# A hybrid attention/SSD trunk layer: later DMA landings in the kernel's own instruction planner, and range checks without a written place on ScalarE

## The chip, the cores and the metric

The kernel runs on one core of a Trainium2 chip. The metric is the device time of one execution in microseconds; the number for a kernel is the median of its runs. A trace comes from one more execution under the hardware profiler, and its span is counted from the first to the last instruction of the kernel.

## What is computed

One layer for 1,024 prompt tokens and 8 x 16 sample tokens, with a model width of 1,024. Cut to what matters here:

```python
def trunk_layer(x, c, conv_buf, h0, attn_fn, norm_g, w_ada, b_ada, w_in, q_norm_g, k_norm_g,
                w_att_proj, conv_w, conv_b, dt_bias, a_log, d_skip, ssd_norm_g, w_ssd_proj, w_out):
    mod = jax.nn.silu(c) @ w_ada + b_ada
    shift, scale, gate = jnp.split(mod[:, None, :], 3, axis=-1)
    h = rms_norm(x, norm_g) * (1 + scale) + shift
    proj = h @ w_in
    q, k, v, z_att, z_ssd, xbc, dt_raw, gates = jnp.split(proj, IN_SPLITS, axis=-1)
    ...
    o_att, k_st, v_st = attn_fn(q, k, v)
    att_branch = (o_att.reshape(b, s, ATT_WIDTH) * jax.nn.silu(z_att)) @ w_att_proj
    xbc, conv_new = causal_dwconv(xbc, conv_buf, conv_w, conv_b)
    ...
    y, h_new = ssd_scan(xs_h, dt, a, bm, cm, h0)
    y = y * jax.nn.silu(z_ssd)
    y = rms_norm(y, ssd_norm_g)
    ssd_branch = y @ w_ssd_proj
    g_att, g_ssd = jnp.split(gates, 2, axis=-1)
    merged = jax.nn.sigmoid(g_att) * att_branch + jax.nn.sigmoid(g_ssd) * ssd_branch
    out = x + gate * (merged @ w_out)
    return out, k_st, v_st, conv_new, h_new
```

All inputs are float32. The attention is chunk-banded (own chunk and the eight chunks of 64 tokens before it), the SSD branch is a Mamba-2 scan in chunks of 64.

## The kernel before, in words

**Arithmetic.** A float32 operand of a large product is cut into two float16 halves: ScalarE writes the high half (L697 for weights, L2198 for operands), VectorE the low half (L698, L2200), and TensorE adds three products, high x high, high x low, low x high (L970, L971, L973 in `dense`; L1023 to L1025 in `dense_tok`; L876 to L878 in `quad_dense`). Since float16 has a small range, each weight and each operand also has its mean square taken: `level` (L689) runs one Square activation on ScalarE with an accumulator, and at the very end all sums are looked at to decide whether a second, general kernel in the same program has to run. It doesn't run with these inputs. Nothing but that last decision waits for a check; only the buffer that it reads stays taken until it has read it.

**Stages.** From 0 to about 83 us the modulation, the normalised input h (`h_hi` L1160, `h_rest` L1165, `h_smp` L1169) and the first product. The weight of that first product (w01) and the three parts of the next are cut by hand there (`w01_high` L1185, `w_high` L1226, `w_low2` L1232), the columns of the modulation come from `mod_cols` L1102, `mod_copy` L1127, `mod_sum` L1108, `mod_c` L1138 and L1139. From there to about 600 us eight attention units (the in-projection of one unit, L1023 to L1025, its evictions L1464, L1465, L1467, its transposes L1521 on TensorE behind a GpSimd multiply L1501). From 600 to about 1264 us sixteen pairs of SSD heads (`dense`, L970 to L973, beside the scan, L1804 to L2151). From 1264 us to the end the two merge gates, the two branch projections and the output projection. These are done with seven products of half-size blocks where the plain way has eight (`quad_dense`, L876 to L878, kept partial sums L895, joined sums L901), for which sums of weight blocks are needed: `quad_sums` loads a weight during the SSD stage (L704), adds its blocks on VectorE (L708) and stores the sums to memory (`sum_d`, L712); they are loaded again just before use (L679). The operands of that stage come back from memory as well (`y_d`, L2281), are multiplied on VectorE (L2286) and cut (L2198, L2200).

**What sets the order.** The code emits all instructions in a written order. A planner in Python, `class Order`, then puts them in the order that is run. `build` makes units of them (one instruction each; up to three matmuls of one tile are merged) with the edges between them. `run` walks through a simulated time: each engine takes, among the units whose inputs are there, first those whose inputs have been there for a safety margin, and of these the one with the smallest number `at`. A unit in the set `fill` has 600 added to its number, so others go first; one in `fast` has 300 taken off. An instruction that the code wraps in `late` is pinned: it gets an edge to the instruction written just before it on its engine, so it keeps that place. For a DMA the plan reckons with a landing of `bus + 700` (L386 to L388). `apply` then fixes the order of every engine by edges, and semaphores between the engines do the rest. So a number in the planner moves no work in or out; it only changes the order in which an engine takes its instructions, and an instruction that has to wait on its engine holds up all that stand behind it.

**Queues.** SP issues all loads, GpSimd the stores to memory that are read again. TensorE has the accumulators `d` (3 slots), `g` (3) and `s` (1) in PSUM: a new tile waits until an old one of its kind has been evicted.

Of the kernel before, what the change touches and what calls it, by code (L numbers as in the profile page):

```python
# [59 lines left out]
SW = 2.0 ** 8  # L60
# [76 lines left out]
        self.arena.release(self.at)  # L137


class Order:  # L140


# [9 lines left out]
    def __init__(self, tc, instructions, pinned, cuts, slow, fill, fast):  # L152
        self.tc, self.slow, self.fill, self.fast = tc, slow, fill, fast
        self.list = [x for x in instructions if x.opcode != "TilePoolBoundary"]
        self.pinned, self.cuts = pinned, cuts

    @staticmethod
    def engine(x):
# [74 lines left out]
    def build(self):  # L233

        units, self.of, last = [], {}, None
        for x in self.list:
            e = self.engine(x)
            if e == "PE":
                small = x.tile_size[0] * x.tile_size[1] < 16384
                out = x.outs[0].bass_ap.tensor.name  # L240
                key = (small, tuple(x.tile_size), "" if small else out)
                if last and last["key"] == key and x.name not in self.cuts and (small or len(last["ins"]) < 3):
                    last["ins"].append(x)
                    self.of[x.name] = last
                    continue
            u = {"eng": e, "ins": [x], "i": len(units), "pred": {}, "succ": [], "key": None}
            if e == "PE":
                u["key"] = key
                last = u
            units.append(u)  # L250
            self.of[x.name] = u
# [4 lines left out]
        for x in self.list:  # L256
            u = self.of[x.name]
            e = u["eng"]
# [4 lines left out]
            for a, w in acc:  # L263
                t, name, r0, r1, c0, c1 = self.region(a)
# [54 lines left out]
    def run(self):  # L319
# [10 lines left out]
        order = {e: [] for e in engines}  # L330
        key = [None]
        bus, low, done = 0.0, 0, [False] * len(units)
# [21 lines left out]
        while n < len(units):  # L354
            best = None
            for e in engines:
# [12 lines left out]
                t = max(free[e], min(c))  # L369
                if best is None or t < best[0]:  # L370
                    best = (t, e)
            assert best, ("no unit can go on", [(e, [(u["i"], u["ins"][0].name) for u in ready[e]][:4]) for e in engines])
            t, e = best
            can = [u for u in ready[e] if u["now"] <= t and u["i"] < low + self.AHEAD]
            sure = [u for u in can if u["sure"] <= t]
# [6 lines left out]
            if u["dma"]:  # L382
                k = nlane[e] % 8
                nlane[e] += 1
                t = max(t, lanes[e][k])
                bus = max(t + 1400, bus) + lat  # L386
                lanes[e][k] = bus + 700
                lat = bus + 700 - t  # L388
            busy = u["busy"]
            if e == "PE":  # L390
                g = u["key"][1]
# [34 lines left out]
def trunk_kernel(ctx: ExitStack, tc: tile.TileContext, h, again):  # L426
# [258 lines left out]
    def level(x, scale, keep=lambda x: x, kind="w"):  # L685

        c, n = meant[kind], x.shape[-1]
        meant[kind] += 1
        keep(nc.scalar.activation(junk[:, :n], x, AF.Square, scale=scale * n ** -0.5, accum_out=sums[:, c:c + 1]))  # L689
# [538 lines left out]
    def w_low2(j):  # L1228
        hi, lo, _ = wsplit[1]
        b = wraw.pop(1 + j)  # L1230
        c = slice(j * 1024, (j + 1) * 1024)
        late(nc.vector.scalar_tensor_tensor(lo.r[:, c], b.ap, SW, hi.ap[:, c], ALU.mult, ALU.subtract))  # L1232
        level(b.ap, SW, late)
        b.free()


    for k in range(KT):
        if k == 0:
# [15 lines left out]
            mod_copy(2)  # L1254
            h_rest(1)
            w01_low(slice(256, 1024))
            level(wraw[0].ap, SW, late)
            wraw.pop(0).free()
            z_mm(0, 0, hlo)
            mod_b(2)  # L1260
# [173 lines left out]
    def h_level():  # L1434
        for k in range(KT):
            yield from pause(6000)
            level(hhi[k].r, 1.0, kind="x")

    urgent.append(ev_first())
    urgent.append(h_level())  # L1440
# [1024 lines left out]
    items.append((out_dense(), [], [], 0.5))  # L2465
    run(items)
    order = Order(tc, list(nc.cur_bb.bb.instructions), pinned, cuts, slow, fill, fast)
    order.build()
    order.run()
    order.apply()  # L2470


# [1866 lines left out]
```

## Time and profile before

| | us |
|---|---|
| median of 3 runs | 1724.09 (1721.27 to 1725.70) |
| the profiled execution's own time | 1723.17 |
| its span in the trace | 1721.4 |
| TensorE matmuls busy | 1678.6 |
| VectorE busy | 1376.6 |
| ScalarE busy | 1058.1 |
| GpSimd busy | 369.1 |

What lies outside the span is 1723.17 - 1721.4 = 1.8 us. In rows of the trace a bracket such as [1.02 <-POOL arena L1501] says that the engine was idle for 1.02 us just before this instruction, and which instruction released it. Names in front of an arrow are the tile that is written: `arena` is the working memory, `d`, `g` and `s` are PSUM tiles. PE is TensorE, DVE is VectorE, ACT is ScalarE, POOL is GpSimd, SP issues the loads.

### The profile page before, as it was taken

The page shows a single profiled execution, that of the slowest core. Times are in us where ns is not written, and L with a number is a line of the kernel's source. Part 1 is how long each engine was busy: PE and PEld are TensorE (multiplying, and loading weights), DVE is VectorE, ACT ScalarE, POOL GpSimd, SP SyncE. Part 2 cuts the span into 40 slices and gives each one's busy share as a digit, 9 for nine tenths or more (in the row PEclk, how much of TensorE's full clock was granted, in tenths as well). Part 3 has the DMA queues.
Part 4 walks back from the last instruction along what each step waited for, and adds up shares of the span by engine and source line. Part 5 has one row for each costly group of instructions (what it writes and reads, how often), then busy time and mean ns, then how long its engine had stood idle before and what let it go on. Part 6 is the DMA issues. An engine that isn't in the chain of part 4 may idle for free. (4 is left out here: it accounts for less than half of the span.)

```text
span 1721.4 us, 36659 instructions
## 1 busy us (share of the span) xinstructions
PE 1678.6 (98%) x14265; PEld 1120.4 (65%) x14265; DVE 1376.6 (80%) x2539; ACT 1058.1 (61%) x2123; POOL 369.1 (21%) x640
## 2 busy tenths in 40 slices
PE   7999999999999999999999999999999999999998
PEld 3556565556565556666666666666657777777776
DVE  6458767878877888889988998997798677888973
ACT  8766556566565668457655765665379665774550
POOL 0133233135133111322321232232212101010000
PEclk9999999999999999999999999999999999999999
DMA  9248789797978687676858867788756866687661
GB/s 383 82 122 210 170 228 225 168 232 187 219 219 192 165 199 221 181 221 199 194 172 263 241 194 238 235 216 268 284 198 221 274 240 234 232 287 264 224 212 65
DMA packets 299249, 369.16 MB, mean 214 GB/s; under 512 B 211692, under 2 KB 213368, under 8 KB 299064
## 3 DMA queue, kind: packets, MB, share of 16 engines
q1 hardware_dynamic: 282040, 307.65, 64.0%
q0 software_dynamic: 17024, 59.06, 9.3%
q8 instruction: 114, 1.87, 0.5%
q14 instruction: 71, 0.58, 0.1%
HBM read 244.08 MB, written 74.06 MB: 185 GB/s over the span
## 5 line engine op out<-in xcount | busy, mean ns | idle before, releaser
L970 PE MATMUL d<-arena 128*128 128x384 f16 x1320 | 432.0, 327 | 4.4 <-DVE arena L1986 2.0
L973 PE MATMUL d<-arena 128*128 128x384 f16 x1320 | 431.5, 327 | 1.2 <-DVE arena L698 1.2
L971 PE MATMUL d<-arena 128*128 128x384 f16 x1320 | 431.3, 327 | 0.0
L689 ACT ACTIVATE arena<-arena 128x1024 bf16<-128x1024 f32 (+4 forms) x217 | 199.2, 918 | 130.1 <-DMA arena<-in_wall_dram 88.2
L698 DVE SCALAR_TENSOR_TENSOR arena<-arena 128x1024 f16<-128x1024 f32 (+2 forms) x157 | 181.8, 1166 | 61.0 <-ACT arena L697 60.5
L697 ACT ACTIVATE arena<-arena 128x1024 f16<-128x1024 f32 (+2 forms) x157 | 155.4, 994 | 83.2 <-DMA arena<-sum_d 40.5
L970 PEld LDWEIGHTS <-arena 128*128 128x128 f16 x1320 | 129.2, 98 | 90.9 <-issue 12.1
L1023 PE MATMUL d<-arena 128*128 128x384 f16 (+1 forms) x568 | 187.0, 329 | 0.0
L1024 PE MATMUL d<-arena 128*128 128x384 f16 (+1 forms) x568 | 186.3, 328 | 0.0
L1025 PE MATMUL d<-arena 128*128 128x384 f16 (+1 forms) x568 | 186.2, 328 | 0.0
L973 PEld LDWEIGHTS <-arena 128*128 128x128 f16 x1320 | 129.0, 98 | 87.8 <-DVE arena L698 1.9
L971 PEld LDWEIGHTS <-arena 128*128 128x128 f16 x1320 | 129.1, 98 | 82.5 <-issue 5.8
L1569 ACT ACTIVATE arena<-arena 128x640 f32<-128x640 f32 (+4 forms) x144 | 100.8, 701 | 63.4 <-DVE arena L1572 63.0
L877 PEld LDWEIGHTS <-arena 128*128 128x128 f16 x1120 | 109.3, 98 | 39.7 <-issue 12.2
L878 PEld LDWEIGHTS <-arena 128*128 128x128 f16 x1120 | 109.3, 98 | 32.4 <-issue 4.3
L876 PEld LDWEIGHTS <-arena 128*128 128x128 f16 x1120 | 109.4, 98 | 29.3 <-issue 1.5
L876 PE MATMUL d<-arena 128*128 128x288 f16 x400 | 114.5, 286 | 5.9 <-DVE arena L901 3.9
L876 PE MATMUL g<-arena 128*128 128x288 f16 x400 | 114.5, 286 | 1.2 <-DVE arena L901 1.2
L877 PE MATMUL g<-arena 128*128 128x288 f16 x400 | 114.5, 286 | 1.2 <-DVE arena L2200 1.2
L877 PE MATMUL d<-arena 128*128 128x288 f16 x400 | 114.5, 286 | 0.2 <-DVE arena L2200 0.2
L878 PE MATMUL g<-arena 128*128 128x288 f16 x400 | 114.5, 286 | 0.0
L878 PE MATMUL d<-arena 128*128 128x288 f16 x400 | 114.5, 286 | 0.0
(277 smaller groups left out, 3521.8 us busy)
## 6 DMA issues: line engine op xcount, KB each, us to landing
arena<-in_quad_dram SPq DMA_DIRECT2D x80, 512.0 KB, 7.0
arena<-in_wall_dram SPq DMA_DIRECT2D x77, 512.0 KB, 5.2
sum_d<-arena POOLq DMA_DIRECT2D x40, 512.0 KB, 4.9
arena<-sum_d SPq DMA_DIRECT2D x40, 512.0 KB, 4.9
arena<-acs_d SPq DMA_DIRECT2D x32, 576.0 KB, 6.2
arena<-in_kc_dram SPq DMA_DIRECT2D x64, 256.0 KB, 4.4
arena<-in_vc_dram SPq DMA_DIRECT2D x64, 256.0 KB, 3.6
arena<-in_wada_dram SPq DMA_DIRECT2D x24, 512.0 KB, 3.7
```

Source lines behind the costliest of these rows:

```text
L689: keep(nc.scalar.activation(junk[:, :n], x, AF.Square, scale=scale * n ** -0.5, accum_out=sums[:, c:c + 1]))
L697: keep(nc.scalar.activation(hi, x, AF.Copy, scale=scale))
L698: keep(nc.vector.scalar_tensor_tensor(lo, x, scale, hi, ALU.mult, ALU.subtract))
L876: nc.tensor.matmul(ps, wh, xh[:, c], start=first and k == 0, stop=False, skip_group_check=not first)
L877: nc.tensor.matmul(ps, wh, xl[:, c], start=False, stop=False, skip_group_check=not first)
L878: nc.tensor.matmul(ps, wl, xh[:, c], start=False, stop=k == 3, skip_group_check=not first)
L970: nc.tensor.matmul(ps, hi.r[:, wc], kh.r[:, tok], start=k == 0, stop=False)
L971: nc.tensor.matmul(ps, hi.r[:, wc], kl.r[:, tok], start=False, stop=False)
L973: nc.tensor.matmul(ps, lo.r[:, wc], kh.r[:, tok], start=False, stop=k == nk - 1)
L1023: nc.tensor.matmul(ps, kh.r[:, tok], wh, start=k == 0, stop=False)
L1024: nc.tensor.matmul(ps, kh.r[:, tok], wl, start=False, stop=False)
L1025: nc.tensor.matmul(ps, kl.r[:, tok], wh, start=False, stop=k == KT - 1)
```

## The change

Three edits, of which only the first two move instructions.

1. In the planner's `run`, a DMA that the plan issues after 600,000 ns (behind the attention stage) lands 1,000 ns later than before in the plan. The transfers themselves are the same.
2. The checks of the startup were pinned behind the instruction written before them (the three parts of the second weight and w01), or free but with their plain number (the eight of h). All twelve are now free and in `fill`, so each gets 600 added to its order number.
3. If the planner finds no unit that can go on, it sets the TensorE units that were ready apart (not merged) and plans again, instead of giving up.

The diff, cut to its core:

```diff
@@ class Order: build
-                if last and last["key"] == key and x.name not in self.cuts and (small or len(last["ins"]) < 3):
+                if last and last["key"] == key and x.name not in self.cuts and x.name not in self.apart and (small or len(last["ins"]) < 3):
@@ class Order: run
-            assert best, ("no unit can go on", [(e, [(u["i"], u["ins"][0].name) for u in ready[e]][:4]) for e in engines])
+            if not best:
+                raise Stuck([x.name for u in ready["PE"] for x in u["ins"]])
...
-                lat = bus + 700 - t
+                lat = bus + 700 - t + (1000.0 if t > 600000.0 else 0.0)
@@ w_low2
-        level(b.ap, SW, late)
+        level(b.ap, SW, lambda x: fill.add(x.ins.name))
@@ the loop over k of the startup
-            level(wraw[0].ap, SW, late)
+            level(wraw[0].ap, SW, lambda x: fill.add(x.ins.name))
@@ h_level
-            level(hhi[k].r, 1.0, kind="x")
+            level(hhi[k].r, 1.0, lambda x: fill.add(x.ins.name), kind="x")
@@ end of trunk_kernel
-    order.build()
-    order.run()
+    while True:
+        order.build()
+        try:
+            order.run()
+            break
+        except Stuck as x:
+            assert not order.apart.issuperset(x.args[0]), "no unit can go on"
+            order.apart.update(x.args[0])
     order.apply()
```

The lines of the changed kernel stand 4 to 5 further down than those of the one before (L689 is L694, L697 is L702, L1465 is L1470), so the rows below are read with that shift. The new order was compared with the old one on all engines. On TensorE it is the same between about 100 and 600 us and in the last 20 us; elsewhere, from 20 to 95 us and from 600 to 1690 us, instructions of all engines have moved.

ScalarE in the startup, at about 59 to 64 us (d_467 and d_496 are the PSUM tiles of the first two in-projection tiles, d_218 is part of the first product), before:

```order
L689 ACTIVATE arena<-arena 128x1024
L689 ACTIVATE arena<-arena 128x1152
L1464 ACTIVATE arena<-d_467 128x256
L1465 ACTIVATE arena<-d_467 128x128
L1467 ACTIVATE arena<-arena 128x256
L1464 ACTIVATE arena<-d_496 128x256
L1465 ACTIVATE arena<-d_496 128x128
L1467 ACTIVATE arena<-arena 128x256
L1311 ACT_TABLE_LOAD
L1311 ACTIVATE arena<-d_218 128x384
```

and the same place now:

```order
L694 ACTIVATE arena<-arena 128x1024
L694 ACTIVATE arena<-arena 128x1152 x2
L1316 ACT_TABLE_LOAD
L1316 ACTIVATE arena<-d_218 128x384
L1469 ACTIVATE arena<-d_467 128x256
L1470 ACTIVATE arena<-d_467 128x128
L1472 ACTIVATE arena<-arena 128x256
L1469 ACTIVATE arena<-d_496 128x256
L1470 ACTIVATE arena<-d_496 128x128
L1472 ACTIVATE arena<-arena 128x256
```

One more check, the table load and the eviction of d_218 now stand ahead of the two evictions of d_467.

VectorE in the SSD stage, at about 875 to 890 us (L708 is an addition of `quad_sums`, L1827 the convolution of a later pair, L2101 to L2123 the scan's sums, s_10628, g_10645 and the other numbers its PSUM tiles), before:

```order
L1827 SCALAR_TENSOR_TENSOR arena<-arena 128x1176
L708 TENSOR_TENSOR arena<-arena 128x512
L1827 SCALAR_TENSOR_TENSOR arena<-arena 128x1176
L2101 SCALAR_TENSOR_TENSOR arena<-arena,s_10628 128x512
L1827 SCALAR_TENSOR_TENSOR arena<-arena 128x1176
L2101 SCALAR_TENSOR_TENSOR arena<-arena,s_10628 128x512
L2101 SCALAR_TENSOR_TENSOR arena<-arena,g_10645 128x128
L2113 TENSOR_TENSOR arena<-arena,g_10645 128x128
L2113 TENSOR_TENSOR arena<-arena,g_10688 128x384
L2114 TENSOR_TENSOR arena<-arena 128x128
L2114 TENSOR_TENSOR arena<-arena 128x384
L2123 TENSOR_TENSOR arena<-arena 128x1024
```

and the same place now:

```order
L1832 SCALAR_TENSOR_TENSOR arena<-arena 128x1176 x3
L2106 SCALAR_TENSOR_TENSOR arena<-arena,s_10628 128x512 x2
L2106 SCALAR_TENSOR_TENSOR arena<-arena,g_10645 128x128
L2118 TENSOR_TENSOR arena<-arena,g_10645 128x128
L2128 TENSOR_TENSOR arena<-arena 128x1024
L2118 TENSOR_TENSOR arena<-arena,g_10688 128x384
L2119 TENSOR_TENSOR arena<-arena 128x128
L2119 TENSOR_TENSOR arena<-arena 128x384
L713 TENSOR_TENSOR arena<-arena 128x512
```

The addition that reads the freshly loaded weight (L708, now L713) stands ten instructions later.

ScalarE in the projections, at about 1459 us (L697 cuts weights, and the last one ahead of the two checks reads a weight sum loaded from `sum_d`; L2198 cuts an operand, s_16464 is a partial sum), before:

```order
L697 ACTIVATE arena<-arena 128x1024
L697 ACTIVATE arena<-arena 128x512
L697 ACTIVATE arena<-arena 128x1024 x2
L689 ACTIVATE arena<-arena 128x576 x2
L2198 ACTIVATE arena<-arena 128x576
L689 ACTIVATE arena<-arena 128x576
L895 ACTIVATE arena<-s_16464 128x288 x2
```

and the same place now:

```order
L702 ACTIVATE arena<-arena 128x1024 x2
L694 ACTIVATE arena<-arena 128x576 x2
L2203 ACTIVATE arena<-arena 128x576
L702 ACTIVATE arena<-arena 128x1024
L694 ACTIVATE arena<-arena 128x576 x2
L2203 ACTIVATE arena<-arena 128x1152 x2
L900 ACTIVATE arena<-s_16464 128x288 x2
```

The cut of that loaded weight sum now stands behind the two checks and the operand cut that it stood ahead of.

More of the change, by code (lines that the diff above doesn't have):

```diff
@@ L137, in free @@
         self.arena.release(self.at)
+class Stuck(Exception):
+    pass
 class Order:
@@ L154, in __init__ @@
         self.list = [x for x in instructions if x.opcode != "TilePoolBoundary"]
-        self.pinned, self.cuts = pinned, cuts
+        self.pinned, self.cuts, self.apart = pinned, cuts, set()
     @staticmethod
```

## Prediction

> **What bounds the kernel now.** I read the page's first part, then the busy times by stage, then TensorE's waits, then what stood ahead of each wait on the engine that released it.
>
> ```profile
> span 1721.4 us, 36659 instructions
> PE 1678.6 (98%) x14265; PEld 1120.4 (65%) x14265; DVE 1376.6 (80%) x2539; ACT 1058.1 (61%) x2123; POOL 369.1 (21%) x640
> ...
> 0.00:83.20 83.20, 70.83 (x483) 40.07 (x484) 49.71 (x74) 66.19 (x121) 8.02 (x20) 1.00 0.63 241
> 83.20:600.00 516.80, 516.00 (x5053) 307.72 (x5052) 387.60 (x1029) 309.07 (x748) 162.88 (x292) 1.00 0.80 195
> 600.00:1264.00 664.00, 654.54 (x5228) 432.45 (x5226) 583.99 (x927) 402.34 (x748) 159.36 (x262) 1.00 0.75 219
> 1264.00:1700.00 436.00, 422.48 (x3388) 328.84 (x3389) 346.95 (x487) 279.76 (x506) 38.84 (x66) 1.00 0.69 234
> 1700.00:1721.40 21.40, 14.76 (x120) 11.27 (x118) 8.40 (x27) 0.78 (x2) 0.00 (x0) 0.95 0.21 74
> ```
>
> The five long rows give a stretch, its length, and then the busy time of PE, PEld, DVE, ACT and POOL, the granted clock, the DMA share and GB/s. TensorE is the bound: 1678.6 of 1721.4 us. The change adds and removes no arithmetic, so all that it can move is TensorE's idle time: by stage 83.20 - 70.83 = 12.4, 0.8, 664.00 - 654.54 = 9.5, 436.00 - 422.48 = 13.5 and 21.40 - 14.76 = 6.6 us, 42.8 in all. The order of TensorE is unchanged from about 100 to 600 us and in the last 20, so what is at stake is the startup and the 9.5 + 13.5 = 23.0 us of the SSD and projection stages. The 0.8 us of idle in the attention stage also says that nothing there can swallow or give back what the startup gains or loses.
>
> **The change part by part: the startup (edit 2).** First the path into the attention stage as it runs now.
>
> ```profile
> 21.98 0.27 ACT L1138 ACTIVATE arena<-g,arena 128x9 f32<-128x9 f32 x1 [0.28 <-PE g L1108]
> ...
> 59.83 1.16 ACT L689 ACTIVATE arena<-arena 128x1152 bf16<-128x1152 f16 x1
> ...
> 61.25 0.27 ACT L1465 ACTIVATE arena<-d 128x128 f32<-128x128 f32 x1
> ...
> 62.58 1.28 ACT L1311 ACT_TABLE_LOAD   x1
> 63.88 0.49 ACT L1311 ACTIVATE arena<-d 128x384 f32<-128x384 f32 x1
> ```
>
> ```profile
> 61.57 0.32 PE L1023 MATMUL d<-arena 128*128 128x384 f16 x1
> ...
> 78.84 0.33 PE L1521 MATMUL g<-arena 128*128 128x128 f32 x1 [1.02 <-POOL arena L1501]
> ```
>
> ```profile
> 76.88 1.90 POOL L1501 TENSOR_TENSOR arena<-arena 128x1024 f32<-128x1024 f32 x1
> ```
>
> TensorE's matmul at 61.57 opens a PSUM tile and needs the slot that L1465 frees at 61.25 + 0.27 = 61.52. In the new order three more things stand ahead of L1465: a check (1.16), the table load (1.28) and the eviction of d_218 (0.49), 2.93 us, less about 0.1 since neighbours on ScalarE overlap. An earlier check now fills the 0.28 us that ScalarE waited at 21.98. So TensorE goes on about 2.9 - 0.1 - 0.3 = 2.5 us later. Behind that, the transposes at 78.84 waited 1.02 us for GpSimd, which ends at 76.88 + 1.90 = 78.78. GpSimd's chain hangs on ScalarE's eviction of the tile begun at 61.57; the two checks that moved ahead no longer stand before that eviction, so it isn't later than now, and TensorE, 2.5 us late, finds the transposes ready. Their 1.02 us go. Startup: 2.5 - 1.0 = **+1.5 us**. The other checks only trade places with work that ScalarE does back to back anyway. If the new order let GpSimd start 2.5 us late too, the cover is gone and it is +2.5; below zero it can't come, since the three instructions really stand there.
>
> The Trainium skill, ScalarE: Activation LUTs, "What ACT_TABLE_LOAD costs", counts a table switch as 1.283 us of load and about 1.38 us of drain, 2.66 in all; by that the startup would lose about 1.4 us more. The trace shows the first part to the digit (1.28) and nothing of the second: the next activation begins 1.30 us after the load.
>
> **The SSD stage (edit 1).** These are the waits of TensorE from 600 to 1264 us that are over 0.6 us, and what stood behind the largest.
>
> ```profile
> 606.48 0.32 PE L970 MATMUL d<-arena 128*128 128x384 f16 x1 [1.42 <-ACT arena L1804]
> ...
> 900.48 0.32 PE L970 MATMUL d<-arena 128*128 128x384 f16 x1 [1.98 <-DVE arena L1986]
> 901.62 0.34 PE L973 MATMUL d<-arena 128*128 128x384 f16 x1 [0.66 <-DVE arena L698]
> ...
> 1132.09 0.82 PE L2060 MATMUL g<-arena 128*128 128x128 f32 x5 [0.63 <-DVE arena L2045]
> ...
> 1209.93 0.32 PE L970 MATMUL d<-arena 128*128 128x384 f16 x1 [1.03 <-ACT arena L1919]
> ...
> 1263.88 1.06 PE L1108 MATMUL g<-arena 128*128 128x9 f32 x8 [3.08 <-ACT arena L2381]
> ```
>
> ```profile
> 875.95 0.33 SPq L704 DMA_DIRECT2D arena<-in_quad_dram  x1
> ```
>
> ```profile
> 880.40 0.69 DVE L708 TENSOR_TENSOR arena<-arena 128x512 f32<-128x512 f32 x1 [4.09 <-DMA arena<-in_quad_dram]
> ...
> 899.88 0.54 DVE L1986 SCALAR_TENSOR_TENSOR arena<-arena,d 128x384 f32<-128x384 f32 x1
> ```
>
> At 876 us VectorE took an addition whose weight had been asked for at 875.95 and stood still for 4.09 us with the convolution and the scan queued behind it; it then had no pause until the eviction at 899.88 that TensorE waits for. In the new order ten instructions whose inputs are there by 879 us go first, so VectorE comes to 899.88 3 to 4 us earlier and both waits (1.98 + 0.66) go: **-2.6**. At 1132 a copy that L2045 follows moves into an earlier wait of VectorE: **-0.6**. At 1210 the eviction L1919 goes ahead of a weight cut of about 1 us (L697): **-1.0**. At 1263.88 the copy of the modulation (L2381) leaves ScalarE's queue five instructions earlier, but its matmuls also stand 12 earlier on TensorE: between -3.1 and -1.1, I take **-2.0**. The wait at 606 has the same instructions around it as before: nothing.
>
> **The projection stage (edit 1).**
>
> ```profile
> 1367.85 0.28 PE L876 MATMUL g<-arena 128*128 128x288 f16 x1 [0.16 <-DVE arena L901]
> ...
> 1370.64 0.28 PE L876 MATMUL d<-arena 128*128 128x288 f16 x1 [1.53 <-DVE arena L901]
> ...
> 1389.59 0.28 PE L876 MATMUL d<-arena 128*128 128x288 f16 x1 [0.78 <-DVE arena L901]
> ...
> 1462.47 0.28 PE L876 MATMUL s<-arena 128*128 128x288 f16 x1 [1.43 <-ACT arena L2198]
> 1463.27 0.28 PE L877 MATMUL s<-arena 128*128 128x288 f16 x1 [0.51 <-DVE arena L2200]
> ...
> 1472.02 0.28 PE L877 MATMUL g<-arena 128*128 128x288 f16 x1 [1.17 <-DVE arena L2200]
> ...
> 1480.06 0.28 PE L876 MATMUL d<-arena 128*128 128x288 f16 x1 [0.65 <-ACT arena L895]
> ...
> 1528.60 0.28 PE L876 MATMUL d<-arena 128*128 128x288 f16 x1 [1.34 <-ACT arena L895]
> ...
> 1543.07 0.28 PE L876 MATMUL g<-arena 128*128 128x288 f16 x1 [1.08 <-DVE arena L901]
> ...
> 1545.73 0.28 PE L876 MATMUL d<-arena 128*128 128x288 f16 x1 [1.40 <-DVE arena L901]
> ```
>
> ```profile
> 1459.32 1.06 ACT L697 ACTIVATE arena<-arena 128x1024 f16<-128x1024 f32 x1 [7.90 <-DMA arena<-sum_d]
> ...
> 1461.76 0.67 ACT L2198 ACTIVATE arena<-arena 128x576 f16<-128x576 f32 x1
> ```
>
> ```profile
> 1463.93 1.41 DVE L2286 SCALAR_TENSOR_TENSOR arena<-arena 128x1152 f32<-128x1152 f32 x1
> ```
>
> ScalarE stood 7.90 us at the cut of a weight sum that had not landed, with the operand cut (L2198) behind it for which TensorE waited at 1462.47. In the new order the operand cut and two checks go first. VectorE in turn takes a multiply of a loaded operand (L2286, 1.41) ahead of the low half, so not all of the four waits from 1462 to 1480 (1.43 + 0.51 + 1.17 + 0.65 = 3.8) goes: **-3.0**. At 1368 the joins (L901) and the low halves change places with a weight's low half: 0.16 + 1.53, **-1.7**; at 1390 the join now stands ahead of three L2286: **-0.8**. At 1528 the copy L895 stands four instructions earlier: **-1.3**. The waits at 1543 and 1546 (2.5) have joins that move ahead of L2200, but lie behind a weight sum that lands late: between -0.6 and -2.5, I take **-1.5**.
>
> **The sum.** Gains 2.6 + 0.6 + 1.0 + 2.0 + 3.0 + 1.7 + 0.8 + 1.3 + 1.5 = 14.5, startup +1.5. But the list only follows waits that exist. The new order is another draw of the same planner, which left 23.0 us of stalls over these two stages, and TensorE reaches each later place up to 14 us earlier. I therefore hold as lasting only what comes from an engine that stood in front of an unlanded transfer (900: 2.6, 1368: 1.7, 1462: 3.0, 1528 to 1546: 2.8, together 10.1); the other 4.4 I write off as likely to come up again elsewhere. And of the 10.1 I take off a fifth, 2.0, for the places where TensorE, now early, outruns a producer. That is -14.5 + 4.4 + 2.0 + 1.5 = **-6.6 us**. Against the profiled execution 1723.17 - 6.6 = 1716.6; the median of before is 0.9 higher and gives 1717.5. I say 1717.
>
> How long a landing takes is the row that speaks for edit 1:
>
> ```profile
> arena<-in_quad_dram SPq DMA_DIRECT2D x80, 512.0 KB, 7.0
> ...
> arena<-sum_d SPq DMA_DIRECT2D x40, 512.0 KB, 4.9
> ```
>
> These medians from issue to landing are 7.0 and 4.9 us. For a lone 512 KB load the plan's formula gives 1400 + 524288/360 + 700 = 3.56 us, and 4.56 with the change: still under both.
>
> The Trainium skill, DMA: Bandwidth & Descriptors, "Anatomy of one DMA", has a fit of 2.0 us plus the bytes at 436 GB/s; 512 KB would then take an estimated 3.2 us, the old formula would be right, and the added 1.0 us would only put consumers later than needed. The rows of 4.9 and 7.0 us don't agree with it, since the transfers here share the queues.
>
> **The rivals.**
>
> *All of it stays gone.* No new stalls: 1723.5 - 14.5 + 1.5 = 1710 to 1711. For it: TensorE's stalls are short, and VectorE has 80 us free of 664 and 89 of 436 to catch up. Against: the same planner's order of before has 23.0 us of them.
>
> *The stalls come up elsewhere*, or the padding does nothing that matters because the landings were late in a handful of places only. Then -14.5 is given back nearly whole: between +1.5 (the startup alone) and about -4, 1720 to 1725. For it: the waits quoted are short and have six different releasers, which looks like chance in the order and not like one cause.
>
> *Slower: the weights of the projections come later.* A plan that believes in landings 1 us later puts each consumer 1 us later, and a weight sum has three transfers in a row (load, store to `sum_d`, load). Where ScalarE already stands for a sum (7.90 us at 1459.32), the cut (L697), the low half (L698) and then TensorE would wait as well. Place: the eight or so products from 1460 us on; price: about 1 us for each of them and for each of the four buffers filled ahead, some 12 us, against gains up to 1390 us of 8.7, halved by the same regrowth to 4.4. Together with the startup 1724 + 12 - 4.4 + 1.5 = 1733. It decides as soon as TensorE waits for L697 or L698 of a weight in that stage; none of the ten waits quoted there is of that kind, and that speaks against it.
>
> **How the numbers follow.** Forecast (1713 to 1719): 0.46. All stays gone: 0.13. Stalls come up elsewhere: 0.28. Slower: 0.13. About 0.3%, 5.2 us, is what a measurement of this kernel can tell from no change. Faster by over that (below 1718.9) are the first two less the edge of the forecast, 0.57; within it the third and that edge, 0.30; slower 0.13. For 8 in 10 the range runs from the lower part of the full gain, 1709, to just beyond the unchanged time, 1727; it leaves out the slower case and a rest of the full gain.
>
> **What the changed profile would show.** Right: TensorE's first in-projection matmul behind the third tile at about 64 us, no wait before the transposes, and about 1.5 us more idle in the startup; no idle of VectorE over 2 us in front of L713 at 876; no wait at 900, less idle than 23.0 in the two later stages by about 8. Wrong: a startup that costs nothing or over 2.5 us; the later stages with 20 us of idle or more at new places; waits for L702 or L703 in the projections.

## The result and the profile after

Each kernel ran six times: 1723.76 us before (1720.77 to 1725.70) and 1712.78 us after (1710.76 to 1716.46). The ratio is 0.9943, with a 95% interval from 0.9928 to 0.9959: the change makes the kernel 0.4 to 0.7% faster, 11.0 us by the medians. The profiled execution has a span of 1710.3 us, 11.1 less than the 1721.4 before. Further down, three executions (1757.95 and 4245.51 us of the kernel with 500 ns, 1956.36 of the one with a load moved) were far slower than the others of their kernel and are left out of its median.

The first lines of the page and the stages of the changed kernel, with the same columns as before (the fourth stage ends 10 us earlier):

```profile
span 1710.3 us, 36659 instructions
PE 1674.1 (98%) x14265; PEld 1122.0 (66%) x14265; DVE 1376.3 (80%) x2539; ACT 1062.7 (62%) x2123; POOL 388.2 (23%) x640
...
0.00:83.20 83.20, 67.93 (x472) 39.34 (x473) 49.62 (x74) 66.23 (x121) 8.27 (x20) 1.00 0.63 241
83.20:600.00 516.80, 515.76 (x5024) 307.62 (x5022) 384.76 (x1024) 308.64 (x747) 163.00 (x292) 1.00 0.81 194
600.00:1264.00 664.00, 658.69 (x5291) 436.52 (x5288) 589.40 (x933) 405.92 (x748) 180.98 (x264) 1.00 0.75 222
1264.00:1690.00 426.00, 418.39 (x3381) 328.36 (x3380) 344.56 (x486) 281.12 (x506) 35.95 (x64) 1.00 0.69 236
```

The instructions are the same. TensorE is idle for longer in the startup (83.20 - 67.93 = 15.3 us against 12.4) and for less behind 600 us (5.3 + 7.6 = 12.9 us against 23.0).

**Where the time went.** Both traces hold 14,265 matmul rows. The start of the n-th row after, less that of the n-th before, says how far TensorE is ahead (minus) or behind (plus) at that place; I read it where the order of TensorE is the same on both sides. "Before" in the table gives the time in the trace before.

| stretch (before, us) | lead at its end, us | change, us | forecast, us |
|---|---|---|---|
| startup, to 102 | +2.11 | +2.1 | +1.5 |
| to 892 | +2.78 | +0.7 | 0 |
| 892 to 919 | -0.19 | -3.0 | -2.6 |
| to 1229 | +0.72 | +0.9 | -1.6 |
| to 1271 | -4.31 | -5.0 | -2.0 |
| to 1424 | -7.47 | -3.2 | -2.5 |
| to 1503 | -9.45 | -2.0 | -3.0 |
| to 1581 | -10.63 | -1.2 | -2.8 |
| to the end | -11.38 | -0.8 | 0 |
| written off for new stalls | | | +6.4 |
| sum (before rounding) | | -11.4 | -6.6 |

**The startup.** ScalarE, then TensorE, at 59 to 64 us after the change:

```profile
59.61 1.16 ACT L694 ACTIVATE arena<-arena 128x1152 bf16<-128x1152 f16 x1
60.68 0.19 ACT L694 ACTIVATION_READ_ACCUMULATOR arena<-arena 128x1 f32 x1
60.90 1.17 ACT L694 ACTIVATE arena<-arena 128x1152 bf16<-128x1152 f16 x1
...
62.18 1.28 ACT L1316 ACT_TABLE_LOAD   x1
63.47 0.49 ACT L1316 ACTIVATE arena<-d 128x384 f32<-128x384 f32 x1
...
64.12 0.28 ACT L1470 ACTIVATE arena<-d 128x128 f32<-128x128 f32 x1
```

```profile
64.46 0.32 PE L1028 MATMUL d<-arena 128*128 128x384 f16 x1 [2.82 <-ACT arena L1470]
```

A check that another check follows takes 60.90 - 59.61 = 1.29 us, not the 1.16 of its own row, since the read of its accumulator stands between the two. (Ahead of an eviction it was 1.16: the check at 59.83 before, the eviction at 60.99.) TensorE starts the tile at 64.46 where it was 61.57.

**Behind 600 us.** The rows of TensorE with the two largest new waits, and two places where it waited before and doesn't now: that of 900 us, and the eight matmuls that waited 3.08 us at 1263.88:

```profile
901.11 0.33 PE L975 MATMUL d<-arena 128*128 128x384 f16 x1
...
1054.13 0.32 PE L975 MATMUL d<-arena 128*128 128x384 f16 x1 [1.67 <-DVE arena L1991]
...
1259.40 0.95 PE L1113 MATMUL g<-arena 128*128 128x9 f32 x8
...
1534.68 0.28 PE L881 MATMUL d<-arena 128*128 128x288 f16 x1 [2.17 <-DVE arena L906]
```

Two waits of before are still there with their old length, 1.17 us at 1462.96 (it was at 1472.02) and 1.36 at 1627.67 (1639.05), and the 1.42 us at 606.48 have become 1.70 at 608.87. VectorE, which stood still at 876 us, now works without a pause from 872.23 to 900.64; its addition (L708, now L713) comes at 884.42.

Where the time comes from is best seen on ScalarE. These are its checks and weight cuts from 600 to 1690 us, before and after; behind the bar stand the busy time, the mean of one in ns, and the idle time just ahead of them with what ended it:

```profile
L689 ACT ACTIVATE arena<-arena 128x576 bf16<-128x576 f32 (+1 forms) x162 | 141.0, 871 | 128.9 <-DMA arena<-in_wall_dram 87.4 <-DVE arena L2355 10.1 <-DMA arena<-in_quad_dram 9.8
L697 ACT ACTIVATE arena<-arena 128x1024 f16<-128x1024 f32 (+1 forms) x124 | 121.3, 984 | 83.0 <-DMA arena<-sum_d 40.5 <-DMA arena<-in_quad_dram 35.7 <-PE g L878 5.1
```

```profile
L694 ACT ACTIVATE arena<-arena 128x576 bf16<-128x576 f32 (+1 forms) x162 | 140.9, 870 | 60.8 <-DMA arena<-in_wall_dram 32.2 <-DVE arena L2291 11.5 <-DVE arena L2360 10.4
L702 ACT ACTIVATE arena<-arena 128x1024 f16<-128x1024 f32 (+1 forms) x124 | 121.4, 984 | 61.8 <-DMA arena<-sum_d 35.3 <-DMA arena<-in_quad_dram 25.9 <-PE g L882 0.3
```

ScalarE does the same work and stands in front of weights that haven't landed for 32.2 us where it was 87.4. All its waits for DMAs in that stretch, added up over the rows of its waits, fall from 203.7 to 115.0 us, and TensorE's waits from 22.9 to 12.6. ScalarE doesn't wait less on the whole: the rows of all its waits there add up to 402.9 us before and 397.8 after. It waits for other engines where it waited for transfers, so the sum for DMAs tells what stood at the front of its queue, not time that was saved.

### The profile page after: what moved, and what is told of

It reads as the page before. It is cut to its first block, busy times and chain, and to the rows that moved or that the text cites. A ratio compares the mean times of both kernels' runs of the same rounds, so it can differ in the third digit from the quotient of the medians.

```text
span 1710.3 us, 36659 instructions
## 1 busy us (share of the span) xinstructions
PE 1674.1 (98%) x14265; PEld 1122.0 (66%) x14265; DVE 1376.3 (80%) x2539; ACT 1062.7 (62%) x2123; POOL 388.2 (23%) x640
## 5 line engine op out<-in xcount | busy, mean ns | idle before, releaser
L694 ACT ACTIVATE arena<-arena 128x1024 bf16<-128x1024 f32 (+4 forms) x217 | 199.1, 918 | 62.2 <-DMA arena<-in_wall_dram 33.0
L703 DVE SCALAR_TENSOR_TENSOR arena<-arena 128x1024 f16<-128x1024 f32 (+2 forms) x157 | 181.7, 1163 | 41.1 <-ACT arena L702 40.7
L702 ACT ACTIVATE arena<-arena 128x1024 f16<-128x1024 f32 (+2 forms) x157 | 155.5, 994 | 61.9 <-DMA arena<-sum_d 35.3
```

The source lines that it names most:

```text
L702: keep(nc.scalar.activation(hi, x, AF.Copy, scale=scale))
L703: keep(nc.vector.scalar_tensor_tensor(lo, x, scale, hi, ALU.mult, ALU.subtract))
```

## The experiments

The ratio is to the kernel before, measured beside each experiment on the same chip, with its interval. The last three columns are sums from 600 to 1690 us of the profiled execution: ScalarE's waits for DMAs, all waits of TensorE, and what TensorE lost to a lower clock. That loss is half of its busy time in the stretches where the granted clock was 0.50.

| kernel | median, us | ratio | ScalarE for DMAs, us | TensorE, us | half clock, us |
|---|---|---|---|---|---|
| before | 1723.76 | 1 | 203.7 | 22.9 | 1.7 |
| the change | 1712.78 | 0.9943 (0.9928 to 0.9959) | 115.0 | 12.6 | 0 |
| edit 1 alone, 1000 ns | 1708.46 | 0.9905 (0.9888 to 0.9923) | 114.8 | 8.9 | 1.7 |
| edit 2 alone | 1726.94 | 1.0011 (0.9994 to 1.0028) | 217.1 | 25.9 | 6.6 |
| three moves by hand | 1720.92 | 0.9979 (0.9965 to 0.9993) | 203.3 | 19.5 | 3.4 |
| margins 20 ns larger | 1721.41 | 0.9989 (0.9970 to 1.0008) | 196.6 | 16.2 | 4.7 |
| margins 20 ns smaller | 1723.62 | 0.9986 (0.9966 to 1.0007) | 193.3 | 19.5 | 5.1 |
| edit 1 with 500 ns | 1718.19 | 0.9967 (0.9950 to 0.9985) | 177.2 | 16.0 | 1.5 |
| edit 1 with 1100 ns | 1715.54 | 0.9932 (0.9912 to 0.9951) | 121.8 | 12.9 | 6.1 |
| edit 1 with 2000 ns | 1731.48 | 1.0033 (1.0019 to 1.0048) | 56.4 | 26.4 | 6.9 |
| 2000 ns, one load moved | 1734.28 | 1.0056 (1.0036 to 1.0076) | 70.5 | 30.3 | 7.0 |
| 2000 ns, own place for checks | 1717.33 | 0.9963 (0.9948 to 0.9978) | 59.2 | 14.7 | 4.1 |
| 2000 ns to 1200 us, then 1000 | 1721.32 | 0.9972 (0.9955 to 0.9989) | 105.3 | 25.4 | 6.5 |
| edit 1 from 100 us on | 1711.55 | 0.9929 (0.9901 to 0.9957) | 115.2 | 12.4 | 0 |

TensorE's waits and the loss at half clock, with the startup's lead at 102 us, give the difference of each span from before to within 3 us; the waits alone don't. For two rows, edit 2 alone (1733.79 us) and the mixture of 2000 and 1000 ns (1728.65), the profiled execution was the slowest of twelve, 7 us over the median; the others lie within 2.3 us of theirs.

### The two edits apart

Edit 1 alone undoes the three lines on the checks:

```diff
-        level(b.ap, SW, lambda x: fill.add(x.ins.name))
+        level(b.ap, SW, late)
-            level(wraw[0].ap, SW, lambda x: fill.add(x.ins.name))
+            level(wraw[0].ap, SW, late)
-            level(hhi[k].r, 1.0, lambda x: fill.add(x.ins.name), kind="x")
+            level(hhi[k].r, 1.0, kind="x")
```

> Edit 1 alone: the landings of the plan are 1000 ns later behind the attention stage, the twelve startup checks stand as they did before the change. Theory A (the two edits act in two separate stages and add up): the startup keeps the time of before, so TensorE is level with before at 100 us, and the later stages keep the gain that the changed kernel shows there, 11.1 + 2.1 = 13.2 us; the span is about 1708 us and the time about 1710. Theory B (the order behind 600 us is a draw that any edit upstream turns over): the startup is level, but the later stages land anywhere between no gain and 14 us, and the waits stand at other places than in the changed kernel.

Edit 2 alone takes the padding away:

```diff
-                lat = bus + 700 - t + (1000.0 if t > 600000.0 else 0.0)
+                lat = bus + 700 - t + (0.0 if t > 600000.0 else 0.0)
```

> Edit 2 alone: the twelve startup checks have no written place and 600 added to their order number, landings are planned as before. Theory A: TensorE starts the in-projection tile behind the third 2.9 us later (64.5 instead of 61.6 us) and is 2.1 us late at 100 us, the later stages have the stalls of before (23 us), so the time is about 2 us above before. Theory B: 2.1 us late at 100 us as well, but the later stages have other stalls, their sum between 15 and 30 us.

Edit 1 alone gives 1708.46 us, the fastest kernel of the study: its interval lies wholly below that of the change. At 102 us TensorE is level with before (+0.11). In its startup the table load stands behind the evictions again, and TensorE has no wait there:

```profile
61.35 0.27 ACT L1470 ACTIVATE arena<-d 128x128 f32<-128x128 f32 x1
...
62.69 1.28 ACT L1316 ACT_TABLE_LOAD   x1
```

Edit 2 alone is the startup's loss and no gain. The tile has the wait of the changed kernel, and TensorE is 2.9 us late at 102 us:

```profile
65.27 0.32 PE L1028 MATMUL d<-arena 128*128 128x384 f16 x1 [2.82 <-ACT arena L1470]
```

Behind 600 us there are 25.9 us of waits where before has 22.9. Its ratio allows from -1.0 to +4.8 us. So the two edits act apart, as Theory A has it. Theory B is answered by the rows themselves: behind 100 us they stand in one order on all five engines (by operation, kind of tile and shape) in the changed kernel and with edit 1 alone, and likewise in before and with edit 2 alone, but for two neighbouring matmuls at 935 us. Edit 2 turns nothing over there. What differs behind 600 us within such a pair is the scatter of executions, not of the order: 12.6 against 8.9 us of TensorE's waits, 22.9 against 25.9, and at the row that is at 1581 us before a lead of 10.6 + 2.1 = 12.7 against 15.3. In the startup edit 2 costs 2.1 to 2.9 us; the kernel with both edits is 4.3 us slower than edit 1 alone by the medians, and where the rest comes from is not shown.

### Three instructions moved by hand

```diff
+    order.move("DVE", "I-9575", "I-10709")
+    order.move("Activation", "I-14417", "I-14329")
+    order.move("Activation", "I-16637", "I-16493")
+    order.move("Activation", "I-16493", "I-16637")
     order.apply()
```

`move` takes one unit out of an engine's finished list and puts it ahead of another; the last two lines together put the weight cut right behind the operand cut.

> The kernel before with three instructions moved by hand in the finished order and nothing else: VectorE's addition at 880 us ten places later, ScalarE's copy of the modulation at 1263 us five places earlier, ScalarE's cut of a weight sum at 1459 us behind the two checks and the operand cut that stood behind it. Theory A (each of these waits was caused by the instruction that stood at the front of its engine's queue): TensorE gains about 2.6 us at 900, up to 3.1 at 1264 and up to 1.4 at 1462, 6 to 7 us in all, and the time is about 1717. Rival (another wait takes the place of each one removed): TensorE is level with before again within 30 us of each place, and the time is that of before within 2 us.

It gives 1720.92 us, 0.2% less than before, between the two theories, and the trace tells the three places apart. At 900 us the start of its rows against before goes from +0.93 to -2.04, a gain of 2.97, and holds that for 300 us. At 1264 it gains 5.0 (from -2.41 to -7.43), and by 1292 all of it is gone (-2.40). These are TensorE's rows there:

```profile
1265.58 0.34 PE L979 MATMUL d<-arena 128*128 128x384 f16 x1 [1.40 <-DVE arena L704]
...
1283.69 1.06 PE L1114 MATMUL g<-arena 128*128 128x9 f32 x8 [1.51 <-ACT arena L2387]
```

It waits for a weight's low half and then, 18 us on, for the next copy of the same kind, 2.9 us in all, and behind the second wait the clock is 0.50 for 3.41 us, another 1.7. In the changed kernel, where the whole plan is new, the gain at 1264 stays. The third move does on ScalarE what it should: the operand cut begins at 1456.56 and not at 1461.76. But VectorE, in its old order, stands for the weight cut that has gone back, and TensorE then waits for the low half behind it (2.09 us, where it had waited 1.43 and 0.51):

```profile
1458.20 1.23 DVE L704 SCALAR_TENSOR_TENSOR arena<-arena 128x1024 f16<-128x1024 f32 x1 [2.63 <-ACT arena L703]
```

```profile
1460.88 0.28 PE L883 MATMUL s<-arena 128*128 128x288 f16 x1 [2.09 <-DVE arena L2206]
```

On the last rows TensorE is 1.38 us ahead. So my reading of the 876 us wait holds by itself; of the two later waits the cause was found too, but the removal of each alone brings nothing.

### Other orders without a reason

```diff
+                m += 20.0 if t > 600000.0 and not v["dma"] else 0.0
                 r = max(r, t)
```

with the padding taken away and the checks as before; the second control has `m -= 20.0`.

> A control without either edit: behind 600 us the planner's safety margins for inputs from the compute engines are 20 ns larger; the plan's landings and the checks are those of before. It changes the order without any reason in the hardware. Theory A (the gain comes from planning with later landings): the stalls of TensorE behind 600 us stay at 23 us within 3, the time within 3 us of before. Theory B (any new order is another draw with a wide spread): they change by more than 5 us either way.

> A second control without either edit: behind 600 us the planner's safety margins for inputs from the compute engines are 20 ns smaller. Theory A: ScalarE's waits for DMAs from 600 to 1690 us stay at 204 us within 25, TensorE's waits there between 16 and 28 us, time 1719 to 1728. Theory B: the time lies outside of that as often as not.

Both times can't be told from before. ScalarE's waits for DMAs stay at 193 to 197 us. TensorE's waits fall to 16.2 and 19.5, lower than I expected for the first, and the loss at half clock rises from 1.7 to 4.7 and 5.1. In these two draws a new order alone is worth nothing that the times show, and the 203.7 to 115 us of ScalarE is the mark of the later landings.

### How much later

Edit 1 alone with 500, 1100 and 2000 ns in the place of 1000.

> As edit 1 alone, but landings are planned 500 ns later instead of 1000. Theory A (planned landings were too early; ScalarE and VectorE stand in front of unlanded transfers, and each 1000 ns takes some of these waits away): ScalarE's waits for DMAs from 600 to 1690 us lie between the 204 us of before and the 115 us of edit 1 alone, 140 to 180; TensorE's waits there between 22.9 and 8.9 us; time 1713 to 1718. Theory B (a lucky order): ScalarE's waits may fall, but the time bears no relation to them, anywhere from 1708 to 1726.

> As edit 1 alone, with 1100 ns instead of 1000: nearly the same reason, another order. Theory A: ScalarE's waits for DMAs from 600 to 1690 us 100 to 125 us, TensorE's waits there 7 to 14 us, time 1706 to 1713. Theory B: TensorE's waits there anywhere from 8 to 25 us, time 1706 to 1724.

> As edit 1 alone, with 2000 ns. Theory A: ScalarE's waits for DMAs fall further, under 100 us; TensorE has 9 to 13 us of waits left to lose there, so the gain flattens: 1704 to 1711. Rival (consumers are put later than needed and weights come late): TensorE waits for the cuts of weights and for joins again, over 15 us, time over 1714. Theory B: anywhere from 1706 to 1724.

ScalarE's waits for DMAs fall with the padding, 203.7, 177.2, 114.8, 121.8, 56.4 us for 0, 500, 1000, 1100 and 2000 ns. The time is 1718, 1708 and 1716 us and then turns: 2000 ns is slower than before. All three expected times of Theory A were missed, the first by 0.2 us, the second by 2.5, the third by its sign. Between 1000 and 1100 ns lie 7 us by the medians, but 4.7 by the ratios, whose intervals overlap. In the traces TensorE's waits differ by 4.0 us and the loss at half clock by 4.4; this is one of its stretches with 1100 ns:

```profile
1071.78:1078.61 6.83, 6.41 (x50) 4.20 (x51) 6.83 (x15) 2.12 (x1) 2.42 (x6) 0.50 0.68 197
```

The median granted clock of all executions says the same, 0.999 with 1000 ns and 0.996 with 1100 and in before. One and the same order, that of the change and of edit 1 alone, also differs by 3.7 us in its waits. So how much of the 7 us is the scatter of the order, Theory B's part, is not shown. The turn at 2000 ns is the rival's, and it sits in one place: TensorE has gained 9.0 us at 1271 us (before), more than in the changed kernel, and is 10.5 behind at 1348. TensorE's rows there:

```profile
1292.50 0.42 PE L881 MATMUL g<-arena 128*128 128x288 f16 x1 [10.49 <-ACT arena L702]
1299.66 0.42 PE L883 MATMUL g<-arena 128*128 128x288 f16 x1 [6.50 <-DVE arena L703]
```

It waits for the high half and then the low half of a weight sum.

### What made 2000 ns slow

SP asked for that sum, the first of the stage, at 1281.89 us, where it was 1267.47 before and 1265.77 in the changed kernel. These are SP's waits from 1250 to 1301 us (the sum of the waits, their number, the longest); it had stood at a load of an attention operand (L2270), and for a check (L694):

```profile
SPq L2270 <- PE g L1107: 19.3, 1, 19.3
SPq L684 <- ACT arena L694: 10.6, 3, 6.5
```

The first try moves the load of the sum ahead of it:

```diff
+    order.move("SP", "I-14427", "I-14836")
     order.apply()
```

> The kernel with landings 2000 ns later, and by hand one load on SP moved: the load of a weight sum that SP issued at 1281.9 us goes ahead of the load of an attention operand, at which SP stood for 19.3 us until TensorE had freed its buffer. Theory A2 (the 10.5 and 6.5 us that TensorE waits for this weight and the next around 1292 to 1300 us come from SP's queue, in which a load that waits holds up all behind it): the sum is asked for at about 1266 us as with 1000 ns, the 10.5 us go, and the time falls by 8 to 17 us to between 1714 and 1723. Rival (the weight was late since its buffer was freed late or since ScalarE cut it late): TensorE still waits about 10 us there and the time stays near 1731.

1734.28 us: the theory of SP's queue falls. The load (L690 here) now stands first and waits itself, for 25.3 us, and for a range check on ScalarE (L700 here):

```profile
SPq L690 <- ACT arena L700: 29.1, 3, 25.3
```

The load takes over a buffer whose last reader is that check. Nor is the late request all. In this run the load issued at 1282.11 landed 4.2 us later, at 1286.3, and ScalarE cut it only at 1293.42, behind four checks and two operand cuts:

```profile
arena<-sum_d SPq DMA_DIRECT2D x1, 512.0 KB, 4.2
```

```profile
1293.42 1.04 ACT L708 ACTIVATE arena<-arena 128x1024 f16<-128x1024 f32 x1
```

So 7.1 of the 12.29 us that TensorE waits there lie between the landing and the cut, in ScalarE's order.

Why the request is late shows on ScalarE too. ScalarE's cut of the weight in that buffer and its check, with 2000 ns:

```profile
1247.50 1.05 ACT L702 ACTIVATE arena<-arena 128x1024 f16<-128x1024 f32 x1
1280.71 1.06 ACT L694 ACTIVATE arena<-arena 128x1024 bf16<-128x1024 f32 x1
```

32 us lie between them. All checks write their squares, which nobody reads, to one place. For the planner these are writes over each other, so the checks keep the order in which they are written in the code, and this one stood behind six checks of operands, from 1270.52 to 1279.91. The second try gives the checks of operands a place of their own:

```diff
+    junk_h = rtile[:, 512:800].bitcast(BF16)
...
-        keep(nc.scalar.activation(junk[:, :n], x, AF.Square, scale=scale * n ** -0.5, accum_out=sums[:, c:c + 1]))
+        out = junk_h if kind == "h" else junk
+        keep(nc.scalar.activation(out[:, :n], x, AF.Square, scale=scale * n ** -0.5, accum_out=sums[:, c:c + 1]))
```

> The kernel with landings 2000 ns later, and one change more: the range checks of operands write the squares that nobody reads to a place of their own. Before, all checks wrote to one place, so the planner kept them in their written order, and the check of a weight stood on ScalarE behind checks of operands written earlier; until it had run, the buffer of that weight could not take the next load. Theory A3 (TensorE's 10.5 and 6.5 us around 1292 to 1300 us come from there: the cut of the weight ended at 1248.5, its check ran at 1280.7, and the sum was asked for at 1281.9): the check runs soon after the cut, the sum is asked for before 1272, TensorE waits under 5 us between 1264 and 1350, and as the whole plan is new the time lies between 1706 and 1722. Rival (a plan with 2000 ns puts the cut late whatever frees the buffer): a wait of over 5 us for a weight stays there, time above 1725.

1717.33 us, 14 us less. SP now asks for the first sum at 1229.70 and for the fourth at 1258.96, and no wait over 3.4 us is left between 1264 and 1350:

```profile
PE g L884 <- ACT arena L2206: 3.4, 1, 3.4
PE g L885 <- DVE arena L2208: 2.2, 2, 1.6
PE s L885 <- DVE arena L2208: 1.6, 1, 1.6
```

That agrees with the check as the cause. It isn't a clean proof, since the edit makes a new plan with other places for everything, the cut's among them; a move of this one check alone was not tried, since the shared place ties it to the checks ahead of it. Nor is the stretch free: the waits add up to 7.2 us, over the 5 that were expected, now for operands, and TensorE still goes from 8.3 us ahead at 1271 us to 2.1 behind at 1348. That is a loss of 10.4 us where it was 19.5.

### Where the padding acts

```diff
-                lat = bus + 700 - t + (1000.0 if t > 600000.0 else 0.0)
+                lat = bus + 700 - t + (0.0 if t < 600000.0 else 2000.0 if t < 1200000.0 else 1000.0)
```

> Edit 1 alone with 2000 ns for loads planned from 600 to 1200 us and 1000 ns behind that. With 2000 ns TensorE had gained 9.0 us at 1264 us and lost all of it behind; with 1000 ns it had gained 4.7 there and 14.4 at the end. Theory A (the gain grows with the planned landing until a load is queued behind one that waits): about 9 us gained at 1264 us and 6 to 10 more behind, 1703 to 1708, no wait of TensorE over 5 us between 1264 and 1350. Theory B (each order is a draw): the second part is turned over as well, anywhere from 1705 to 1725.

and, apart from it, `1000.0 if t > 100000.0`:

> Edit 1 alone with the 1000 ns from 100 us on instead of 600, so in the attention stage too. TensorE has 0.8 us of idle there with the old landings, so there is nothing to gain. Theory A: level with before at 600 us within 2 us, and a gain behind it that is some part of 14 us since the order there starts from another state: 1706 to 1716. Rival (loads put later cost as soon as there is no wait to remove): TensorE late by 3 us or more at 600 us.

The mixture fails: 1721.32 us. Up to 1215 us the rows of all engines stand in the order of 2000 ns, so that its lead at 1271 us is 4.8, and not 9, has no cause in the plan: it is the scatter of executions (a wait of 2.72 us at 753 us is in this trace alone). Behind 1271 us TensorE waits 6.5 and 4.7 us for the same two halves of a weight sum, and for the same reason. The check runs at 1282.19, 29 us behind its cut (1251.69 to 1252.74), SP waits for it and asks for the sum at 1283.37:

```profile
SPq L684 <- ACT arena L694: 30.3, 3, 21.9
```

The sum lands 4.1 us later, at 1287.5, and is cut at 1293.93. With 1000 ns from 100 us on the time is 1711.55, in the range of Theory A: TensorE is 0.8 us late at 585 us, nothing gained and nothing lost in the attention stage, and the gain behind it is there.

## Why the prediction was right, and where its steps were off

The forecast was 1717 us, 6.6 less than the profiled execution; measured were 1712.78 and a span 11.1 us shorter. The startup loses and the later stages gain, as forecast, and edit 1 is the cause of the gain. That the gain comes from engines that no longer stand in front of transfers is shown at 900 us; the largest single gain, at 1264 us, has another source. By steps:

- **Startup, +1.5 forecast, +2.1 measured.** TensorE comes 2.9 us late, not 2.5, above all because the two checks in a row hold ScalarE for 1.29 and 1.28 us and not for the 1.16 of a row; of the 0.28 us credited to an earlier check 0.20 arrived (ScalarE's check that began at 58.63 now begins at 58.43). The 1.02 us behind GpSimd went, as reckoned, since GpSimd's end didn't move (the multiply that began at 76.88 begins at 76.93). A wait for GpSimd of 0.24 us at 96.44 is new.
- **900 us, -2.6 forecast, -3.0 measured.** No wait at either place, and VectorE doesn't stand still at 876; the hand-moved kernel, with a gain of 2.97, shows that this one instruction is the cause.
- **To 1229 us, -1.6 forecast, +0.9 measured.** The waits at 1132 and 1210 went, but a wait of 1.67 us stands at 1054, and smaller ones elsewhere. This is what the write-off was for.
- **1264 us, -2.0 forecast, -5.0 measured.** The size of this term failed most. I took 2.0 of the 3.08 us of wait; all 3.08 went, and a loss that I hadn't counted went with it. These are TensorE's busy time and granted clock (the 0.72) in the 6 us behind that wait, before and after:

```profile
1264.00:1270.00 6.00, 6.00 (x34) 3.30 (x35) 6.00 (x8) 4.78 (x7) 1.62 (x3) 0.72 0.73 237
```

```profile
1264.00:1270.00 6.00, 6.00 (x42) 3.41 (x41) 6.00 (x13) 5.94 (x13) 1.08 (x2) 1.00 0.52 175
```

  A clock of 0.72 over 6 us is 1.7 us of work not done. I had seen only the wait. Nor did this gain come from a transfer: before, the copy that TensorE waited for stood on ScalarE behind four checks that ran back to back from 1260.15 on; now it stands ahead of them. Before and after:

```profile
1262.57 0.68 ACT L689 ACTIVATE arena<-arena 128x576 bf16<-128x576 f32 x1
...
1263.25 0.58 ACT L2381 ACTIVATE arena<-g 128x512 f32<-128x512 f32 x1
```

```profile
1257.62 0.57 ACT L2386 ACTIVATE arena<-g 128x512 f32<-128x512 f32 x1
```

  I had written this gain off as one that would come up again elsewhere, and it was the largest that lasted.
- **To 1424 us, -2.5 forecast, -3.2 measured; to 1581 us, -5.8 forecast, -3.2 measured.** The waits at 1368 to 1390 are gone; in the stretches that had 3.8 us each, 1462 to 1480 and 1528 to 1546, there are still 2.6 and 2.2 us. Of the 2.6, 1.17 is a wait of before that stayed; the 2.2 are one wait for a join, the releaser of two of the three before.
- **The write-off, +6.4 forecast.** Too large. Without it the forecast would have been 1710, and 1712.78 lies nearer to that than to 1717. The reason given for it, that the order is another draw, is not borne out: the times of the two controls can't be told from before, and the waits of one and the same order scatter by 3 to 4 us between executions. That the sum came within 5 us is in part luck: terms too small by 3.0 (1264 us) and a write-off too large stand against gains that were put too high, by 2.5 up to 1229 us and by 2.6 behind 1424.

Of the rivals, the slower one (weights of the projections late) didn't happen at 1000 ns. At 2000 there are waits of its kind, for L702 and L703, at 1292 to 1300 us and not from 1460 on, where the rival put them. One part is its own mechanism, a cut that stands behind other work when its weight has landed; the other I hadn't seen, a check that keeps a buffer.

The fit that the prediction takes from the Trainium skill, DMA: Bandwidth & Descriptors, "Anatomy of one DMA", is given there for DMAs that GpSimd issues. The loads in the two rows beside it are issued by SP, so their 4.9 and 7.0 us say nothing against that fit, and that shared queues are the reason was not tested.

## What to carry to other kernels

A planner that reckons with too early landings puts engines in front of data that isn't there; the sum of one engine's waits for DMAs answers to the planner's number, where the time also answers to chance. It is no measure of time: with 2000 ns it was the lowest and the kernel among the slowest. A control that changes the order for no reason, and one order measured twice, show how large chance is. Before a difference of a few us is put down to the order, compare the granted clock of the two traces. Work that nobody waits for, like a range check, still decides when a buffer comes free, and a scratch place that is written and never read ties all who write to it into one order.

## What the runs showed of the hardware

A wait of TensorE can cost more than its length. After the 3.08 us at 1264 us before, the granted clock was at 0.72 over the next 6 us; with 2000 ns, after 10.49 and 6.50 us of wait, it was 0.64 in the 18 us of the waits and 0.50 for four us after them:

```profile
1282.00:1300.00 18.00, 1.00 (x5) 0.38 (x5) 16.36 (x18) 16.93 (x31) 9.19 (x10) 0.64 0.30 88
1300.00:1304.00 4.00, 4.00 (x19) 2.49 (x18) 4.00 (x5) 2.98 (x6) 0.00 (x0) 0.50 0.66 210
1304.00:1320.00 16.00, 16.00 (x132) 12.79 (x131) 10.81 (x15) 13.01 (x26) 1.71 (x3) 1.00 0.75 241
```

With three moves by hand, a wait of only 1.51 us was followed by 0.70 in the four us from 1286 on:

```profile
1286.00:1290.00 4.00, 4.00 (x25) 2.75 (x24) 2.08 (x4) 3.94 (x9) 0.00 (x0) 0.70 0.59 141
```

The 1.98 us at 900 us before were followed by a clock of 1.00, as were the 2.17 us at 1534.68 in the changed kernel.

In the fourteen traces there are 26 stretches with a clock of 0.50 between 100 us and 10 us before the end. They last 3.41, 6.83 or 17.07 us, and each begins while TensorE waits or within 1.9 us of the end of a wait of over 1 us. A stretch of 3.41 us in which TensorE is busy costs 1.7 us.

The Trainium skill, TensorE: Matmul & The Clock Gate, "Part 1: The HAM clock gate", tells of half the clock after an idle window of about 3.4 us and of about 3.4 us of work until it is full again. The half clock and the time to come back agree with these rows; the length of the wait doesn't, since 1.51 us were enough in one place and 1.98 were not in another. What decides that is not settled here.
